# Routing weights applied at the experts' PSUM eviction, and an adding scatter into one row per token

## The chip, the cores and the metric

The kernel runs on one core of one Trainium2 chip. The metric is the device time of one execution in microseconds, and the figure for a kernel is the median of its runs. The profile shows one execution, taken by the hardware profiler. Its engines are PE (TensorE matmul), PEld (TensorE weight load), DVE (VectorE), ACT (ScalarE), POOL (GpSimd) and SP (SyncE, which issues most DMAs); 16 DMA engines move the data of all queues.

## The reference

One decoder block over 512 tokens of width 2048, in float32: a normalisation, a projection, 8 heads of forgetting attention beside 8 heads of chunkwise retention, gates, an output projection and a residual `h`. Behind it stands a mixture of 32 experts in 4 groups: each token takes one group, and in it the two best experts. Only this part is touched by the change:

```python
top_p, top_i = lax.top_k(e_prob, TOP_K)
top_p = top_p / jnp.sum(top_p, axis=-1, keepdims=True)
weights = p_group[:, None] * top_p
expert_id = g_sel[:, None] * EXPERTS_PER_GROUP + top_i
...
return (jax.nn.silu(xi @ w1[e]) * (xi @ w3[e])) @ w2[e]
...
yb = lax.map(expert_block, (xb, blk_expert)).reshape(cap, d) * buf_w[:, None]
return jnp.zeros((t_tok + 1, d), h.dtype).at[buf_tok].add(yb)[:t_tok]
```

The block's output is the normalised sum of `h` and this mixture. Each expert's matrices `w1`, `w3` (2048x512) and `w2` (512x2048) are 12.6 MB in float32, and all 32 are used.

## The kernel before

The program has four stages. Projections with both branches, then the output projection and the residual, run up to about 1420 us. The router follows, up to about 1441 us: it computes logits, the best group (`gm`, `ohg`), the best and second-best expert as one-hot arrays (`A1`, `A2`), and each token's rank in its expert (`rank1`, line 678). Then come the 32 experts, one after the other, and at the end the function `combine`, which adds everything up per token, normalises and stores.

**Experts.** The main loop is in lines 903 to 935. For each expert, `prep` (line 715) builds a 0/1 selection matrix `S` of tokens to 64 slots on POOL (expert 0 on DVE), and gathers the tokens' activations with matmuls of `h3` against `S` (line 737), in two halves; the halves are separate steps of a generator. A small matmul of `S` with the table `aux` (line 724, tile `ax`) carries a few numbers per slot: the token's inverse norm `rs`, its number, and whether this expert is its second choice. From them DVE computes `idx`, the row of the scatter (lines 755 to 760). `gemm1` (line 768) multiplies by `w1` and `w3`, `gated` (line 784) turns and gates the result, `gemm2` (line 798) multiplies by `w2`. The two halves of its output, `y`, are 128x512 tiles in PSUM: one is copied to `ysb` by ACT (line 815), the other by DVE (line 813). Then POOL issues an indirect DMA, the scatter (line 826), which writes the filled slots' rows of 4 KB into the DRAM tensor `ybuf`. That has 2 x 512 rows: row 2k holds token k's output of its best expert, row 2k+1 that of its second. Empty slots get a row number past the bound and are dropped. `ybuf` is set to zero earlier, by eight DMAs of 1 MB, one behind each attention head (line 332). The tile `ysb` has one buffer.

The last expert doesn't pass through `ybuf`. Its output is weighted (`wsl`), split in two float32r parts in `ys`, and put on the tokens by matmuls with the transposed selection `sT` (lines 817 to 823 and 960).

**Weights' stream.** SP loads the experts' matrices in pieces of 2 MB, six for each expert, into eight buffers that go round (`buffer`, line 702). The load of a piece waits until the matmuls on the buffer's last content are done. At the second-last expert two buffers are kept out of the round for `fw` and `ys` (lines 921 to 923).

**Routing weights.** `mixing` (line 870) computes them (`wt`: two numbers per token) on DVE with two Exp on ACT. The loop calls it at expert 12 and holds it behind that expert's gating. Its results are first read by `diagonals` (line 927) and by the last expert.

**combine** (line 940). Four loads of 2 MB bring `ybuf` back (lines 944 to 945); they stand on SP's queue behind the last weights and wait for the last scatter. For each of 4 tiles of 128 tokens and each of 4 blocks `c` of 512 columns, PE adds into PSUM three bfloat16 parts of `h` (line 957), the second choice's row times a diagonal matrix of its weight (line 959; left out for `c` = 0) and the last expert (line 960). DVE adds the first choice's row times its weight (line 961), and for `c` = 0 the second choice's as well (line 964). ACT sums the squares (line 966), POOL multiplies half of the blocks by the final norm's weight (line 968), DVE computes the inverse root in 13 small steps for each token tile, DVE and ACT scale (lines 976 and 978), and SP stores.

**Order.** On PE and SP the order of work is that of the program text. On DVE, ACT and POOL a planner sets the order, from a simulated timeline.

Of the kernel before, what the change touches and what calls it, by code (L numbers as in the profile page):

```python
# [11 lines left out]
F32 = mybir.dt.float32  # L12
F32R = mybir.dt.float32r
BF = mybir.dt.bfloat16
# [112 lines left out]
def hybrid_block(ctx, tc, a, out):  # L127
# [5 lines left out]
    def b3(ap, *shape):  # L133
        return ap.to_broadcast([P] + list(shape))
# [28 lines left out]
    c_d = dram.tile([H, T], F32, name="c_d")  # L163
    ybuf = dram.tile([2 * T, D], F32, name="ybuf")

# [126 lines left out]
    def fox_head(h, v):  # L292
# [38 lines left out]
        with tc.issue_after(done.ins):  # L331
            nc.scalar.dma_start(ybuf[h * P:(h + 1) * P].rearrange("p (a b) -> p a b", b=P),
                                zero[:, None, :].to_broadcast([P, D // P, P]))

# [130 lines left out]
    with pool("mtmp", 2, reuse_waits="tile") as mt:  # L465
        for j in range(KT):
            hi, lo = unit("br", j, after=done[3] if j == 1 else None)
            gs, bs = [], []
            for n in range(2):
# [4 lines left out]
                for k in range(H):  # L474
# [30 lines left out]
    tok2 = rp[0].tile([P, NT], F32, name="tok2")  # L505
    nc.gpsimd.iota(tok2, pattern=[[4 * P, NT]], base=0, channel_multiplier=0,
                   allow_small_or_imprecise_dtypes=True)
    par2 = rp[0].tile([P, NT], F32, name="par2")
    nc.gpsimd.iota(par2, pattern=[[0, NT]], base=0, channel_multiplier=4,
                   allow_small_or_imprecise_dtypes=True)  # L510
    aux = rp[0].tile([P, NT, 40], BF, name="aux")
    nc.gpsimd.memset(aux[:, :, 5:8], -8192.0)
    nc.gpsimd.tensor_copy(aux[:, :, 3], tok2)
# [176 lines left out]
    nc.gpsimd.dma_start(fwk, a["norm_final_w"].rearrange("o (k p) -> (o k) p", p=P))  # L690
    auxw = rp[0].tile([P, NT, 3], BF, name="auxw")

# [18 lines left out]
    rowbase = rp[0].tile([P, 1], F32, name="rowbase")  # L711
    nc.gpsimd.memset(rowbase[:SLOTS], 8192.0)
    nc.gpsimd.memset(rowbase[SLOTS:], 8193.0)

    def prep(rsel, is2, eng, late=False):

        S = cp.tile([P, NT, P], BF, name="S")
        for t in range(NT):
            i = eng.tensor_scalar(S[:, t], slot1.rearrange("p a b -> p (a b)"), rsel[:, t:t + 1], None,  # L719
                                  op0=OP.is_equal)  # L720
        gathering.append(i.ins)
        ax = psY.tile([P, 40], F32, name="ax", tag="y")
        for t in range(NT):
            nc.tensor.matmul(ax, S[:, t], aux[:, t], start=(t == 0), stop=(t == NT - 1))  # L724
        rs = cp.tile([P, 1], F32, name="rs", bufs=3)
        nc.vector.reduce_sum(rs, ax[:, 0:3], axis=AX.X)  # L726
        xs = cp.tile([P, KT, SLOTS], F32, name="xs")
        blk = [xs, rs, None]
        for g in range(2):
            if g:  # L730
                yield blk
            ks = slice(8 * g, 8 * g + 8)
            gp = psG.tile([P, 8, SLOTS], F32, name="gp")
            for d in range(8):
                for t in range(NT):
                    for i in range(3):
                        nc.tensor.matmul(gp[:, d], h3[i][:, t, (8 * g + d) * P:(8 * g + d + 1) * P],  # L737
                                         S[:, t, :SLOTS], start=(t == 0 and i == 0),
                                         stop=(t == NT - 1 and i == 2))
            nc.vector.tensor_mul(xs[:, ks], gp, b3(nfw[:, ks, None], 8, SLOTS))  # L740
        if late:
            ws = psY.tile([P, 3], F32, name="ws", tag="y")
            for t in range(NT):
                nc.tensor.matmul(ws, S[:, t], auxw[:, t], start=(t == 0), stop=(t == NT - 1))
            wsl = cp.tile([P, 1], F32, name="wsl", bufs=1)
            nc.vector.reduce_sum(wsl, ws, axis=AX.X)
            sp = psR.tile([P, NT, P], F32, name="tr")
            for t in range(NT):
                nc.tensor.matmul(sp[:, t], S[:, t], idb, start=True, stop=True)
            sT = cp.tile([P, NT, P], F32R, name="sT", bufs=1)  # L750
            nc.scalar.copy(sT, sp)
            blk[2] = wsl, sT
            yield blk
            return
        ix = cp.tile([P, 1], F32, name="ix", bufs=3)
        idx = cp.tile([P, 1], I32, name="idx", bufs=3)
        nc.vector.reduce_sum(ix, ax[:, 3:6], axis=AX.X)
        nc.vector.tensor_add(ix, ix, rowbase)
        nc.vector.scalar_tensor_tensor(idx, is2(ax[:, 8:40]), 2.0, ix, op0=OP.mult, op1=OP.add)
        blk[2] = idx  # L760
        yield blk
# [6 lines left out]
    def gemm1(blk, pieces, between=None):  # L768

        xs, rs, _ = blk  # L770
        acc = psA.tile([P, DE], F32, name="ab")
        for g in range(2):
            w = [next(pieces), next(pieces)]
            if g and between is not None:
                next(between)
            for kk in range(8):
                k = 8 * g + kk
                halves_mm(acc, xs[:, k], [w[m][:, kk * DE:(kk + 1) * DE] for m in range(2)],
                          k == 0, k == KT - 1)
        sb = cp.tile([P, DE], F32, name="ab", bufs=1)  # L780
        nc.scalar.activation(sb, acc, AF.Copy, scale=rs)  # L781
        return sb
# [15 lines left out]
    def gemm2(blk, pieces, ys=None):  # L798

        gs, (_, _, idx) = blk  # L800
        if ys is not None:
            wsl, sT = idx
        else:
            ysb = yp[0].tile([P, 2, DE], F32, name="ysb")
        w = [next(pieces), next(pieces)]
        for q in range(2):
# [4 lines left out]
            if ys is None:  # L811
                if q:
                    nc.vector.tensor_copy(ysb[:, q], y)
                else:
                    nc.scalar.copy(ysb[:, q], y)
                continue
# [7 lines left out]
        if ys is not None:  # L824
            return sT
        nc.gpsimd.indirect_dma_start(
            out=ybuf.rearrange("r (m n) -> (r m) n", m=2),
            out_offset=IndirectOffsetOnAxis(ap=idx[:, :1], axis=0),
            in_=ysb.rearrange("p q n -> p (q n)"), in_offset=None, bounds_check=4 * T - 1, oob_is_err=False)

# [39 lines left out]
    def mixing():  # L870
# [23 lines left out]
        for n in range(2):  # L894
            nc.vector.tensor_mul(wt[:, n], wt[:, n], wsum)
        wl, w2 = f("wl", NT), f("wl2", NT)
        nc.vector.tensor_mul(wl, wt[:, 0], A1.rearrange("p t g j -> p t (g j)")[:, :, NE - 1])
        nc.vector.tensor_mul(w2, wt[:, 1], A2[:, :, NE - 1])
        nc.vector.tensor_add(wl, wl, w2)
        split3(auxw, wl)  # L900
        return wt

    yp.append(scC.enter_context(pool("yout", 1, reuse_waits="tile")))
    nxt = prep_e(0)
    cur = next(nxt)
    for e in range(NE):
        sb = gemm1(cur, pieces_of(a["wM"][e], 0), None if e else nxt)
        if e == 8:
            with tc.issue_after(last_ins[-1].ins):
                nblk, eid, sta, en, it = extra_blocks()  # L910
        if e == 12:
            with tc.issue_after(last_ins[-1].ins):
                wtf = mixing()
        was = cur
# [11 lines left out]

    def diagonals():

        dgs = cp.tile([P, NT, P], F32, name="dgs", tag="ab", bufs=1)
        for t in range(NT):  # L930
            nc.gpsimd.tensor_scalar_mul(dgs[:, t], ident, wtf[:, 1, t:t + 1])
        return dgs

    dgs = diagonals()
    sT = gemm2((gs, was), pieces_of(a["wM"][NE - 1], 1), ys)


    yv = ybuf.rearrange("(t p k) d -> t p k d", p=P, k=2)

    def combine(dgs, first=False):  # L940

        def load_y(t):

            yb = buffer((P, 2, D))
            nc.sync.dma_start(yb, yv[t])
            return yb[:, 0], yb[:, 1]

        ybs = [load_y(t) for t in range(NT)] if first else None
        for t in range(NT):
            r, y1 = ybs[t] if first else load_y(t)  # L950
            dg = dgs[:, t]
            ss = small.tile([P, 4], F32, name="ss4")
            for c in (2, 3, 0, 1):
                cs = slice(c * T, (c + 1) * T)
                pr = psY.tile([P, T], F32, name="y") if c % 2 else psA.tile([P, T], F32, name="ab")
                for i in range(3):
                    nc.tensor.matmul(pr, idb, h3[i][:, t, cs], start=(i == 0), stop=False)
                if c:
                    nc.tensor.matmul(pr, dg, y1[:, cs], start=False, stop=False)
                nc.tensor.matmul(pr, sT[:, t], ys[:, cs], start=False, stop=True)  # L960
                nc.vector.scalar_tensor_tensor(r[:, cs], r[:, cs], wtf[:, 0, t:t + 1], pr,  # L961
                                               op0=OP.mult, op1=OP.add)
                if not c:
                    nc.vector.scalar_tensor_tensor(r[:, cs], y1[:, cs], wtf[:, 1, t:t + 1], r[:, cs],  # L964
                                                   op0=OP.mult, op1=OP.add)
                nc.scalar.activation(pr, r[:, cs], AF.Square, accum_out=ss[:, c:c + 1])
# [15 lines left out]

    combine(dgs, True)


    n_extra = nc.values_load(nblk[0:1, 0:1], min_val=0, max_val=MAXBLK)  # L986
    with tc.If(n_extra > 0):
        with tc.For_i(0, n_extra, 1):
# [27 lines left out]
            gemm2((gated(gemm1(blk, pieces_of(we, 0))), blk), pieces_of(we, 1))  # L1016
        combine(diagonals())
    scC.close()
# [70 lines left out]
```

## Time and profile before

| | |
|---|---|
| median of 3 runs | 2460.95 us (2460.93 to 2462.9) |
| the profiled execution | 2456.61 us, its span 2454.9 us |
| mean granted TensorE clock | 0.989 |
| busy share of the span | PE 96%, PEld 66%, DVE 30%, ACT 19%, POOL 10% |
| HBM read, written | 562.72 MB, 37.24 MB |
| experts' weights | 192 loads of 2048 KB |
| scatters | 31, median 10.5 us from issue to landing |
| loads of `ybuf` | 4 of 2048 KB |

The busy share of PE is high in every stage, so it doesn't tell which stage is bound by what: a matmul that waits a little before it starts still leaves PE nearly full. The busy share of the DMA engines tells the stages apart, and it is read per stretch of time. Times inside the span are given from its start.

### The profile page before, as it was taken

The page shows a single profiled execution, that of the slowest core. Times are in us where ns is not written, and L with a number is a line of the kernel's source. Part 1 is how long each engine was busy: PE and PEld are TensorE (multiplying, and loading weights), DVE is VectorE, ACT ScalarE, POOL GpSimd, SP SyncE. Part 2 cuts the span into 40 slices and gives each one's busy share as a digit, 9 for nine tenths or more (in the row PEclk, how much of TensorE's full clock was granted, in tenths as well). Part 3 has the DMA queues.
Part 4 walks back from the last instruction along what each step waited for, and adds up shares of the span by engine and source line. Part 5 has one row for each costly group of instructions (what it writes and reads, how often), then busy time and mean ns, then how long its engine had stood idle before and what let it go on. Part 6 is the DMA issues. An engine that isn't in the chain of part 4 may idle for free. (4 is left out here: it accounts for less than half of the span.)

```text
span 2454.9 us, 36000 instructions
## 1 busy us (share of the span) xinstructions
PE 2357.7 (96%) x16112; PEld 1618.9 (66%) x16114; DVE 725.4 (30%) x1269; ACT 471.3 (19%) x586; POOL 237.1 (10%) x330
## 2 busy tenths in 40 slices
PE   8999999999999999999999979999999999999996
PEld 6888888888888888888888854444444444444443
DVE  4444445543442222244433231101010000000005
ACT  5212223223222222232223310000010000000004
POOL 0000000100100000001003221111111111111102
PEclk9999999999999999999999989999999999999998
DMA  7233324232223332344432379999999999999995
GB/s 290 98 107 126 110 98 142 78 112 73 108 78 129 129 124 105 116 157 150 150 109 102 137 306 404 426 425 426 425 426 426 425 426 423 424 426 424 426 398 219
DMA packets 71439, 594.22 MB, mean 242 GB/s; under 512 B 8792, under 2 KB 25240, under 8 KB 37616
## 3 DMA queue, kind: packets, MB, share of 16 engines
q1 hardware_dynamic: 40320, 549.48, 54.8%
q0 software_dynamic: 9840, 25.61, 3.1%
q10 hardware_dynamic: 21120, 16.78, 2.1%
q8 instruction: 128, 2.10, 0.3%
q14 instruction: 31, 0.25, 0.0%
HBM read 562.72 MB, written 37.24 MB: 244 GB/s over the span
## 5 line engine op out<-in xcount | busy, mean ns | idle before, releaser
L766 PE MATMUL ab<-wraw,xs 128*64 128x512 f32 x2048 | 480.2, 602 | 40.6 <-DMA wraw<-in_wM_dram 38.9
L225 PE MATMUL acc<-xh,whl 128*128 128x512 f32 x1152 | 453.2, 393 | 0.0
L227 PE MATMUL acc<-xh,whl 128*128 128x512 f32 x1152 | 453.2, 393 | 0.0
L226 PE MATMUL acc<-xl,whl 128*128 128x512 f32 x1152 | 452.7, 393 | 0.0
L766 PEld LDWEIGHTS ab<-wraw,xs 128*64 128x64 f32 x2048 | 159.8, 139 | 353.9 <-issue 283.5
L96 ACT CAST whl<-wraw 128x2048 fp32r<-128x2048 f32 (+1 forms) x122 | 228.0, 1869 | 779.9 <-PE acc L227 412.5
L97 DVE TENSOR_TENSOR whl<-wraw,whl 128x2048 fp32r<-128x2048 f32 (+1 forms) x122 | 275.3, 2257 | 201.4 <-ACT whl L96 201.0
L226 PEld LDWEIGHTS acc<-xl,whl 128*128 128x128 f32 x1152 | 216.4, 188 | 46.6 <-issue 1.4
L227 PEld LDWEIGHTS acc<-xh,whl 128*128 128x128 f32 x1152 | 216.4, 188 | 45.7 <-issue 1.4
L225 PEld LDWEIGHTS acc<-xh,whl 128*128 128x128 f32 x1152 | 216.4, 188 | 45.6 <-issue 0.5
L766 PE MATMUL y<-wraw,gs 128*64 128x512 f32 x1024 | 229.1, 599 | 0.0
L737 PE MATMUL gp<-S,h 128*128 128x64 bf16 x6144 | 193.1, 193 | 16.1 <-issue 16.1
L737 PEld LDWEIGHTS <-h 128*128 128x128 bf16 x6144 | 187.9, 98 | 18.4 <-issue 18.1
L766 PEld LDWEIGHTS y<-wraw,gs 128*64 128x64 f32 x1024 | 71.1, 137 | 131.6 <-issue 129.9
L781 ACT ACTIVATE ab<-ab,rs 128x512 f32<-128x512 f32 x32 | 22.0, 688 | 619.6 <-PE ab L766 596.3
L726 DVE TENSOR_REDUCE rs<-ax 128x1 f32<-128x3 f32 x32 | 5.1, 160 | 459.1 <-PE ax L724 459.1
L719 POOL TENSOR_SCALAR S<-slot,rank 128x128 bf16<-128x128 f32 x124 | 73.3, 601 | 607.1 <-PE gp L737 600.5
L242 PE MATMUL acc<-whl,xh 128*128 128x512 f32 x256 | 101.6, 401 | 6.2 <-ACT xh L201 6.2
L243 PE MATMUL acc<-whl,xh 128*128 128x512 f32 x256 | 102.5, 400 | 0.9 <-DVE whl L97 0.9
L595 PE MATMUL acc<-whl,mh 128*128 128x512 f32 x256 | 100.4, 392 | 0.0
L596 PE MATMUL acc<-whl,mh 128*128 128x512 f32 x256 | 100.2, 391 | 0.0
L479 PE MATMUL acc<-oh,whl 128*128 128x512 f32 x256 | 99.4, 390 | 0.6 <-DVE whl L85 0.6
(303 smaller groups left out, 2061.9 us busy)
## 6 DMA issues: line engine op xcount, KB each, us to landing
wraw<-in_wM_dram SPq DMA_DIRECT2D x192, 2048.0 KB, 27.8
wraw<-in_wA_dram SPq DMA_DIRECT2D x59, 2048.0 KB, 7.7
ybuf<-zero ACTq DMA_DIRECT2D x8, 1024.0 KB, 5.9
gate<-gs ACTq DMA_DIRECT2D x32, 256.0 KB, 2.0
g<-gate POOLq DMA_DIRECT2D x32, 256.0 KB, 2.9
wraw<-ybuf SPq DMA_DIRECT2D x4, 2048.0 KB, 17.7
xt<-in_x_dram SPq DMA_DIRECT2D x4, 1024.0 KB, 6.9
hc<-in_x_dram POOLq DMA_DIRECT2D x4, 1024.0 KB, 5.5
```

The source lines that it names most:

```text
L96: nc.scalar.copy(hi[:, c], w[:, c])
L97: nc.vector.tensor_sub(lo[:, c], w[:, c], hi[:, c].bitcast(F32))
L225: nc.tensor.matmul(acc, wh, xh[:, k], start=(k == 0), stop=False)
L226: nc.tensor.matmul(acc, wh, xl[:, k], start=False, stop=False)
L227: nc.tensor.matmul(acc, wl, xh[:, k], start=False, stop=(k == KT - 1))
L242: nc.tensor.matmul(accs[t], xh[:, k, s], wh, start=(k == 0), stop=False)
L243: nc.tensor.matmul(accs[t], xh[:, k, s], wl, start=False, stop=False)
L479: nc.tensor.matmul(b, wl, oh[i], start=False, stop=(k == H - 1))
L595: nc.tensor.matmul(accs[t], mh[k][:, s], wh, start=(k == 0), stop=False)
L596: nc.tensor.matmul(accs[t], mh[k][:, s], wl, start=False, stop=False)
L737: nc.tensor.matmul(gp[:, d], h3[i][:, t, (8 * g + d) * P:(8 * g + d + 1) * P], S[:, t, :SLOTS], start=(t == 0 and i == 0), stop=(t == NT - ...
L766: nc.tensor.matmul(acc[m * SLOTS:(m + 1) * SLOTS], st, w[m], start=first, stop=last)
```

## The change

The DRAM tensor `ybuf` has one row per token instead of two. The scatter is issued with `compute_op=OP.add`: a row is added to what stands in `ybuf` instead of overwriting it. The two evictions of `y` multiply by the routing weight of each slot, `wsl`. So that the weight is there in time, `mixing` is called ahead of expert 0's first product; it writes the first choice's weight and the difference of the two weights, in three bfloat16 parts each, to six new columns of `aux`, and the small matmul `ax` carries them to the slots. That matmul moves from ahead of the gather's first half to ahead of its second half, and the steps on its result move behind the gather. `idx` loses the factor for the second choice. In `combine`, two loads of 2 MB replace four, the diagonal matrices with their matmuls and DVE's line 964 go, and DVE's line 961 becomes a plain addition. The zeroing of `ybuf` is halved: it stands behind every second head.

```diff
-    ybuf = dram.tile([2 * T, D], F32, name="ybuf")
+    ybuf = dram.tile([T, D], F32, name="ybuf")
...
-            nc.scalar.dma_start(ybuf[h * P:(h + 1) * P].rearrange("p (a b) -> p a b", b=P),
-                                zero[:, None, :].to_broadcast([P, D // P, P]))
+            if h % 2:
+                nc.scalar.dma_start(ybuf[h // 2 * P:(h // 2 + 1) * P].rearrange("p (a b) -> p a b", b=P),
+                                    zero[:, None, :].to_broadcast([P, D // P, P]))
...
-    aux = rp[0].tile([P, NT, 40], BF, name="aux")
+    aux = rp[0].tile([P, NT, 46], BF, name="aux")
...
-        ax = psY.tile([P, 40], F32, name="ax", tag="y")
-        for t in range(NT):
-            nc.tensor.matmul(ax, S[:, t], aux[:, t], start=(t == 0), stop=(t == NT - 1))
-        rs = cp.tile([P, 1], F32, name="rs", bufs=3)
-        nc.vector.reduce_sum(rs, ax[:, 0:3], axis=AX.X)
...
             if g:
                 yield blk
+                ax = psY.tile([P, 46], F32, name="ax", tag="y")
+                for t in range(NT):
+                    nc.tensor.matmul(ax, S[:, t], aux[:, t], start=(t == 0), stop=(t == NT - 1))
...
+        nc.vector.reduce_sum(rs, ax[:, 0:3], axis=AX.X)
+        nc.vector.reduce_sum(wd, ax[:, 40:46].rearrange("p (a b) -> p a b", a=2), axis=AX.X)
+        nc.vector.scalar_tensor_tensor(wsl, is2(ax[:, 8:40]), wd[:, 1:2], wd[:, 0:1], op0=OP.mult, op1=OP.add)
...
-        nc.vector.reduce_sum(ix, ax[:, 3:6], axis=AX.X)
-        nc.vector.tensor_add(ix, ix, rowbase)
-        nc.vector.scalar_tensor_tensor(idx, is2(ax[:, 8:40]), 2.0, ix, op0=OP.mult, op1=OP.add)
+            nc.vector.reduce_sum(ix, ax[:, 3:6], axis=AX.X)
+            nc.vector.tensor_add(idx, ix, rowbase)
...
-                    nc.vector.tensor_copy(ysb[:, q], y)
+                    nc.vector.tensor_scalar_mul(ysb[:, q], y, wsl)
                 else:
-                    nc.scalar.copy(ysb[:, q], y)
+                    nc.scalar.activation(ysb[:, q], y, AF.Copy, scale=wsl)
...
-            in_=ysb.rearrange("p q n -> p (q n)"), in_offset=None, bounds_check=4 * T - 1, oob_is_err=False)
+            in_=ysb.rearrange("p q n -> p (q n)"), in_offset=None, bounds_check=2 * T - 1, oob_is_err=False,
+            compute_op=OP.add)
...
-        wl, w2 = f("wl", NT), f("wl2", NT)
-        nc.vector.tensor_mul(wl, wt[:, 0], A1.rearrange("p t g j -> p t (g j)")[:, :, NE - 1])
-        nc.vector.tensor_mul(w2, wt[:, 1], A2[:, :, NE - 1])
-        nc.vector.tensor_add(wl, wl, w2)
-        split3(auxw, wl)
-        return wt
+        nc.vector.tensor_sub(wt[:, 1], wt[:, 1], wt[:, 0])
+        for n in range(2):
+            split3(aux[:, :, 40 + 3 * n:43 + 3 * n], wt[:, n])
...
     cur = next(nxt)
+    mixing()
     for e in range(NE):
         sb = gemm1(cur, pieces_of(a["wM"][e], 0), None if e else nxt)
...
-        if e == 12:
-            with tc.issue_after(last_ins[-1].ins):
-                wtf = mixing()
...
-    dgs = diagonals()
     sT = gemm2((gs, was), pieces_of(a["wM"][NE - 1], 1), ys)
...
+        for t in range(0, NT, 2):
             yb = buffer((P, 2, D))
-            nc.sync.dma_start(yb, yv[t])
-            return yb[:, 0], yb[:, 1]
+            nc.sync.dma_start(yb, ybuf.rearrange("(t p) d -> p t d", p=P)[:, t:t + 2])
+            ybs += [yb[:, 0], yb[:, 1]]
...
-                if c:
-                    nc.tensor.matmul(pr, dg, y1[:, cs], start=False, stop=False)
                 nc.tensor.matmul(pr, sT[:, t], ys[:, cs], start=False, stop=True)
-                nc.vector.scalar_tensor_tensor(r[:, cs], r[:, cs], wtf[:, 0, t:t + 1], pr,
-                                               op0=OP.mult, op1=OP.add)
-                if not c:
-                    nc.vector.scalar_tensor_tensor(r[:, cs], y1[:, cs], wtf[:, 1, t:t + 1], r[:, cs],
-                                                   op0=OP.mult, op1=OP.add)
+                nc.vector.tensor_add(r[:, cs], r[:, cs], pr)
```

## Rows read from the trace of the kernel before

**Rows 1.** The page, part 2: the span in 40 equal slices.

```profile
DMA  7233324232223332344432379999999999999995
```

**Rows 2.** Busy time by stretch: stretch, length, PE, PEld, DVE, ACT, POOL, PEclk, DMA share, GB/s.

```profile
1440.00:1460.00 20.00, 16.20 (x242) 10.54 (x244) 4.29 (x15) 0.00 (x0) 3.71 (x7) 0.83 0.29 104
...
2200.00:2300.00 100.00, 92.19 (x916) 41.94 (x914) 9.13 (x24) 4.97 (x9) 10.17 (x15) 0.98 1.01 425
2300.00:2350.00 50.00, 45.30 (x544) 22.73 (x542) 5.39 (x15) 3.32 (x6) 3.40 (x5) 1.00 0.96 404
2350.00:2370.00 20.00, 19.49 (x184) 8.56 (x181) 1.40 (x3) 0.77 (x2) 0.97 (x1) 1.00 0.96 390
...
2411.00:2448.00 37.00, 25.03 (x88) 11.01 (x88) 32.47 (x83) 18.77 (x44) 11.28 (x8) 0.89 0.34 138
```

**Rows 3.** Timeline, PE, from 2390 us: the last half of the last `gemm1`.

```profile
2390.08 7.08 PE L766 MATMUL ab<-wraw,xs 128*64 128x512 f32 x30 [2.33 <-DMA wraw<-in_wM_dram]
```

**Rows 4.** DMA queues from 1500 to 2380 us: packets, MB, share of 16 engines; issues.

```profile
q1 hardware_dynamic: 24974, 363.65, 97.5%
q0 software_dynamic: 4176, 7.64, 2.3%
...
ybuf<-ysb,idx POOLq DMA_INDIRECT x29, 10.5
```

**Rows 5.** Groups of instructions from 2411 to 2455 us: count, busy us, mean ns, idle.

```profile
L959 PE MATMUL y<-wraw,dgs 128*128 128x512 f32 x16 | 8.2, 592 | 0.0
L976 DVE SCALAR_TENSOR_TENSOR wraw<-wraw,rs_w 128x512 f32<-128x512 f32 x8 | 6.7, 873 | 0.1
...
L961 DVE SCALAR_TENSOR_TENSOR wraw<-wraw,wt,ab 128x512 f32<-128x512 f32 x8 | 5.9, 742 | 2.1 <-PE ab L960 1.9
L961 DVE SCALAR_TENSOR_TENSOR wraw<-wraw,wt,y 128x512 f32<-128x512 f32 x8 | 5.9, 737 | 0.6 <-PE y L960 0.6
...
L964 DVE SCALAR_TENSOR_TENSOR wraw<-wraw,wt 128x512 f32<-128x512 f32 x4 | 5.1, 1275 | 0.0
```

**Rows 6.** Timeline: an ACT eviction with a scale, a DVE product from PSUM.

```profile
1466.65 0.69 ACT L781 ACTIVATE ab<-ab,rs 128x512 f32<-128x512 f32 x1 [31.57 <-PE ab L766]
...
1788.87 0.69 DVE L740 TENSOR_TENSOR xs<-gp,nfw 128x512 f32<-128x512 f32 x1 [2.19 <-PE gp L737]
```

**Rows 7.** Timeline: `ybuf`'s loads on SP, and the first addition on DVE.

```profile
2392.53 4.98 SPq L945 DMA_DIRECT2D wraw<-ybuf  x4
...
2413.15 0.75 DVE L961 SCALAR_TENSOR_TENSOR wraw<-wraw,wt,ab 128x512 f32<-128x512 f32 x1 [1.92 <-PE ab L960]
```

**Rows 8.** Timeline: `mixing` beside expert 12, first and last of 27 on DVE, and ACT.

```profile
1790.09 0.16 DVE L874 TENSOR_TENSOR pgx<-L,fm1m 128x16 f32<-128x16 f32 x1
...
1796.50 0.17 DVE L686 TENSOR_TENSOR auxw<-s,auxw 128x4 bf16<-128x4 f32 x1
...
1789.74 1.28 ACT L875 ACT_TABLE_LOAD   x1
```

**Rows 9.** Timeline of the start of expert 0, PE and DVE.

```profile
1441.85 0.29 DVE L678 SCALAR_TENSOR_TENSOR rank<-rk,A 128x128 f32<-128x128 f32 x1 [0.67 <-PE rk L676]
...
1447.91 0.69 DVE L740 TENSOR_TENSOR xs<-gp,nfw 128x512 f32<-128x512 f32 x1 [3.74 <-PE gp L737]
...
1442.52 0.92 PE L724 MATMUL ax<-aux,S 128*128 128x40 bf16 x4 [0.77 <-DVE S L719]
1443.26 4.61 PE L737 MATMUL gp<-S,h 128*128 128x64 bf16 x96
...
1455.68 2.97 PE L737 MATMUL gp<-S,h 128*128 128x64 bf16 x96
```

**Rows 10.** Timeline: a scatter on POOL, and the next write to `ysb` on ACT.

```profile
1771.85 1.04 POOL L826 DMA_INDIRECT ybuf<-ysb,idx  x1 [5.99 <-issue]
...
1795.77 0.59 ACT L815 COPY ysb<-y 128x512 f32<-128x512 f32 x1 [3.74 <-PE y L766]
```

**Rows 11.** Landing times of the 18 scatters from 1440 to 2000 us (line 826).

```profile
DMA to landing us min/median/max: 10.1/10.4/11.4
```

More of the change, by code (lines that the diff above doesn't have):

```diff
@@ L505, in hybrid_block @@
     tok2 = rp[0].tile([P, NT], F32, name="tok2")
-    nc.gpsimd.iota(tok2, pattern=[[4 * P, NT]], base=0, channel_multiplier=0,
+    nc.gpsimd.iota(tok2, pattern=[[2 * P, NT]], base=0, channel_multiplier=0,
                    allow_small_or_imprecise_dtypes=True)
     par2 = rp[0].tile([P, NT], F32, name="par2")
-    nc.gpsimd.iota(par2, pattern=[[0, NT]], base=0, channel_multiplier=4,
+    nc.gpsimd.iota(par2, pattern=[[0, NT]], base=0, channel_multiplier=2,
                    allow_small_or_imprecise_dtypes=True)
-    aux = rp[0].tile([P, NT, 40], BF, name="aux")
-    nc.gpsimd.memset(aux[:, :, 5:8], -8192.0)
+    aux = rp[0].tile([P, NT, 46], BF, name="aux")
+    nc.gpsimd.memset(aux[:, :, 5:8], -4096.0)
     nc.gpsimd.tensor_copy(aux[:, :, 3], tok2)
@@ L690, in hybrid_block @@
     nc.gpsimd.dma_start(fwk, a["norm_final_w"].rearrange("o (k p) -> (o k) p", p=P))
-    auxw = rp[0].tile([P, NT, 3], BF, name="auxw")
     cp = scC.enter_context(pool("cx", 2, reuse_waits="tile"))
@@ L711, in hybrid_block @@
     rowbase = rp[0].tile([P, 1], F32, name="rowbase")
-    nc.gpsimd.memset(rowbase[:SLOTS], 8192.0)
-    nc.gpsimd.memset(rowbase[SLOTS:], 8193.0)
+    nc.gpsimd.memset(rowbase[:SLOTS], 4096.0)
+    nc.gpsimd.memset(rowbase[SLOTS:], 4097.0)
     def prep(rsel, is2, eng, late=False):
@@ L721, in prep @@
         gathering.append(i.ins)
-        ax = psY.tile([P, 40], F32, name="ax", tag="y")
-        for t in range(NT):
-            nc.tensor.matmul(ax, S[:, t], aux[:, t], start=(t == 0), stop=(t == NT - 1))
-        rs = cp.tile([P, 1], F32, name="rs", bufs=3)
-        nc.vector.reduce_sum(rs, ax[:, 0:3], axis=AX.X)
         xs = cp.tile([P, KT, SLOTS], F32, name="xs")
-        blk = [xs, rs, None]
+        blk = [xs, None, None, None]
         for g in range(2):
@@ L740, in prep @@
             nc.vector.tensor_mul(xs[:, ks], gp, b3(nfw[:, ks, None], 8, SLOTS))
-        if late:
[L742 to L746, printed above, removed]
+        rs = cp.tile([P, 1], F32, name="rs", bufs=3)
+        ix = cp.tile([P, 1], F32, name="ix", bufs=1)
+        idx = cp.tile([P, 1], I32, name="idx", bufs=3)
+        wd = cp.tile([P, 2], F32, name="wd", bufs=1)
+        wsl = cp.tile([P, 1], F32, name="wsl", bufs=3)
+        nc.vector.reduce_sum(rs, ax[:, 0:3], axis=AX.X)
+        nc.vector.reduce_sum(wd, ax[:, 40:46].rearrange("p (a b) -> p a b", a=2), axis=AX.X)
+        nc.vector.scalar_tensor_tensor(wsl, is2(ax[:, 8:40]), wd[:, 1:2], wd[:, 0:1], op0=OP.mult, op1=OP.add)
+        blk[1:] = rs, wsl, idx
+        if late:
             sp = psR.tile([P, NT, P], F32, name="tr")
@@ L751, in prep @@
             nc.scalar.copy(sT, sp)
[L752 to L756, printed above, removed]
-        nc.vector.reduce_sum(ix, ax[:, 3:6], axis=AX.X)
-        nc.vector.tensor_add(ix, ix, rowbase)
-        nc.vector.scalar_tensor_tensor(idx, is2(ax[:, 8:40]), 2.0, ix, op0=OP.mult, op1=OP.add)
-        blk[2] = idx
+            blk[3] = sT
+        else:
+            nc.vector.reduce_sum(ix, ax[:, 3:6], axis=AX.X)
+            nc.vector.tensor_add(idx, ix, rowbase)
         yield blk
@@ L768, in gemm1 @@
     def gemm1(blk, pieces, between=None):
-        xs, rs, _ = blk
+        xs = blk[0]
         acc = psA.tile([P, DE], F32, name="ab")
@@ L780, in gemm1 @@
         sb = cp.tile([P, DE], F32, name="ab", bufs=1)
-        nc.scalar.activation(sb, acc, AF.Copy, scale=rs)
+        nc.scalar.activation(sb, acc, AF.Copy, scale=blk[1])
         return sb
@@ L798, in gemm2 @@
     def gemm2(blk, pieces, ys=None):
[L800 to L803, printed above, removed]
+        gs, (_, _, wsl, idx) = blk
+        if ys is None:
             ysb = yp[0].tile([P, 2, DE], F32, name="ysb")
@@ L824, in gemm2 @@
         if ys is not None:
-            return sT
+            return idx
         nc.gpsimd.indirect_dma_start(
@@ L925, in hybrid_block, with combine @@
     spread_fw(fw)
-    def diagonals():
-        dgs = cp.tile([P, NT, P], F32, name="dgs", tag="ab", bufs=1)
-        for t in range(NT):
-            nc.gpsimd.tensor_scalar_mul(dgs[:, t], ident, wtf[:, 1, t:t + 1])
-        return dgs
-    dgs = diagonals()
[L935 to L944, printed above, removed]
-            nc.sync.dma_start(yb, yv[t])
-            return yb[:, 0], yb[:, 1]
[L948 to L951, printed above, removed]
+    sT = gemm2((gs, was), pieces_of(a["wM"][NE - 1], 1), ys)
+    def combine():
+        ybs = []
+        for t in range(0, NT, 2):
+            yb = buffer((P, 2, D))
+            nc.sync.dma_start(yb, ybuf.rearrange("(t p) d -> p t d", p=P)[:, t:t + 2])
+            ybs += [yb[:, 0], yb[:, 1]]
+        for t in range(NT):
+            r = ybs[t]
             ss = small.tile([P, 4], F32, name="ss4")
@@ L981, in combine @@
                 nc.sync.dma_start(out[t * P:(t + 1) * P, cs], r[:, cs])
-    combine(dgs, True)
+    combine()
     n_extra = nc.values_load(nblk[0:1, 0:1], min_val=0, max_val=MAXBLK)
@@ L1016, in hybrid_block @@
             gemm2((gated(gemm1(blk, pieces_of(we, 0))), blk), pieces_of(we, 1))
-        combine(diagonals())
+        combine()
     scC.close()
```

## The prediction

> **What bounds the kernel now.** I read the slices of the span first. The busy share of the DMA engines is 1 to 4 tenths up to the router, but for the first slice, and then 9 tenths almost to the end [rows 1]. So there are two kernels in one, and the change touches only the second. The stretches come next: in a hundred microseconds of the experts' stage the DMA share is 1.01 at 425 GB/s, while PE is busy for 92 of 100 us [rows 2]. PE has some 8% to spare there, DVE 90% and ACT 95%. The stage lasts as long as its bytes take. At its start it is different: in the first 20 us the DMA share is 0.29 [rows 2], since the buffers are full and PE has not yet begun to free them. A late start of PE there moves everything behind it. That the stage ends on a DMA shows in the last half of the last `gemm1`, which begins at 2390.08 us after 2.33 us of waiting for a weight [rows 3]. From there some 65 us are left: the last expert's arithmetic, and from 2411 us on `combine`, where DVE is busy 32.5 of 37 us, PE 25 and the DMA engines a third of the time [rows 2]. There DVE is the bound.
>
> So an edit counts if it changes the bytes of the experts' stage, the start of PE at expert 0, or DVE's work in `combine`. The change does something to all three.
>
> **The scatter adds.** The queues of 1500 to 2380 us [rows 4] are the main view. The weights' queue moved 363.65 MB at 97.5% of 880 us, 858 us, so 424 GB/s. The scatters' queue moved 7.64 MB in 29 scatters, 0.263 MB each, at 2.3%, 20.2 us, or 0.70 us each. The shares add up to a full stage: a scatter isn't hidden beside the weights but takes their place. To add, something has to read the old row: the scatter's bytes are now read twice and written once. The trace has no adding DMA, so I bound the cost. Below: nothing, if an engine fetches the old row while it is busy with the other side of the transfer. Above: the old row is fetched and the sum written as passes of their own, two more scatters' worth, 2 x 0.70 = 1.40 us. Between the ends I take one more read of the same bytes at the rate at which the weights are read from the same memory, 0.263 MB / 424 GB/s = 0.62 us, since a read from HBM into the engines is what these rows show most of. 30 of the 31 scatters are issued before 2390 us: 30 x 0.62 = 18.6 us. From 2300 to 2370 us the DMA share is 0.96 [rows 2], so 2.8 us are free there, and the two or three scatters in it can put about 1 us into them. **+17.6 us**, with ends at 0 and 30 x 1.40 = +42 us.
>
> The Trainium skill, "Collectives: The Full Stack", in the section on the bandwidth ceiling, says that an add in a DMA costs no cycles of its own but needs two source reads on the same read ring, and measures a reduction at 1/1.93 of a copy's rate. By that ratio each scatter would cost 0.93 x 0.62 = 0.58 us more, the term +17 us; no run here shows it yet.
>
> **combine.** DVE loses line 964, 5.1 us in four instructions [rows 5]. They run at 1.275 us, 0.74 being the price of the like line 961, so they were stretched by something beside them. Line 961, 16 times at 0.74 us, becomes an addition of a PSUM operand; the nearest row, a product of the same shape from PSUM, takes 0.69 us [rows 6]: 16 x 0.05 = 0.8 us. Together 5.9 us from an engine that is the bound, but in the first microseconds it waits for PE [rows 5, 7], so I take **-5.5 us**. If only the unstretched price comes back (4 x 0.74) and nothing else, -3; if the other stretched lines relax too (line 976 runs at 0.873), up to -8. PE loses the 24 passes of line 959, 16 of them at 8.2 us busy, so some 12 of its 25 us [rows 2, 5]: nothing, as DVE ends later. What is late next is still DVE, with some 26 us, ahead of ACT's 19 [rows 2].
>
> **Loads of ybuf.** Two of 2 MB instead of four. The first tile's data still comes with the first 2 MB; it was issued at 2392.53 us and DVE first adds at 2413.15 [rows 7]. The saved 4 MB lie behind it, under a DMA share of 0.34 [rows 2]: nothing. The cover is some 3 us: if the last scatter lands later, this load starts later, but then alone on the engines, with 2.1 MB / 424 GB/s = 5 us for 2 MB.
>
> **mixing moved to the front.** Beside expert 12 it took 27 DVE instructions from 1790.09 to 1796.67 us, and a table load of 1.28 us on ACT [rows 8]. The new one has three less for the last expert's weight, one subtraction and four splits more: 29, some 7 us. At the start DVE is free from about 1443 us on but for 0.7 us at 1447.9, and the first reader is now `ax` of expert 0 ahead of the gather's second half at 1455.68 us [rows 9]. 12 us of room for 7: nothing. PE's queue waits behind that `ax`, so what is over the room would be paid in full; and if the planner put all of it ahead of `rank`, the start would be 7 us later. On the other side `ax` itself leaves the front of the first gather: 1443.26 - 1442.52 = 0.74 us [rows 9] earlier. I take **0**, with ends at -0.7 and +7.
>
> **At nothing.** The evictions with a scale: ACT does one in 0.69 us [rows 6] against 0.59 for the copy [rows 10], and PE is not the bound. The new reductions for `wsl`: some four DVE instructions of 0.16 us for each expert, under 90% of idle DVE. `ax` in its new place: it shares PSUM buffers with `y`, and its readers are done about 1 us after the gather, well before the second `y`. The table of `aux`: 46 columns for 40. The halved zeroing: ACT's queue in the attention, at a DMA share of 2 to 4 tenths [rows 1]. Also gone are the four POOL products of `diagonals`, off the path.
>
> **Sum.** 17.6 - 5.5 + 0 = +12.1 us. On the profiled execution, 2456.6 us (span 2454.9 and 1.7 around it), that is 2468.7. That execution is 4.3 us below the median of the runs, 2460.95, so I put the difference on the median: **2473 us**. The limit of what a measurement of this kernel can tell from no change is about 0.2%, 4.9 us.
>
> **Rivals.**
> *The added read is hidden.* If an engine reads the old row beside its write, only `combine` is left: 2460.95 - 5.5 = 2455.5 us, faster. For it speaks that reading and writing are different directions; against it that in [rows 4] the scatters and the weights, which go in opposite directions, already share the engines' time without overlap. With a part of the read hidden, 0 to 10 us of the 17.6, the result is between 2456 and 2466.
> *Two passes more.* 42 - 1 - 5.5 = +35 us: 2496. For it speaks that the scatter is already dearer for its bytes than the weights (0.70 against 0.62 us); against it, nothing seen.
> *The landing becomes a wait.* `ysb` has one buffer; ACT writes it again 24 us after the scatter's issue [rows 10], and a scatter lands in 10.4 us [rows 11]. A landing up to twice as long is covered. Beyond 24 us ACT waits, PE's next `y` behind it, and after PE's spare time, 8% of 30 us, each microsecond is paid 30 times. At 30 us of landing: (30 - 24 - 2.4) x 30 = 108 us, 2580. It takes an adding row that blocks its queue for a round trip.
> The Trainium skill, "DMA: Bandwidth & Descriptors", section on two DMAs through the same engine, reports that the second of two adding packets read stale data when it directly followed the first; so they don't wait for each other's round trip, which speaks against this case. No run here shows it.
> *The start.* mixing ahead of the first gather: 2473 + 7 = 2480.
>
> **How the numbers follow.** One more read: 0.55, with its own band of 2466 (the start 0.7 earlier, `combine` at -8, the read 15% cheaper) to 2481 (the late start). Hidden read: 0.13, half of it under 2456. Partly hidden: 0.11. Two passes: 0.16, from 2482 to 2502. The landing: 0.05. Faster by over 0.2% is the whole hidden read and a bit of its neighbour: 0.11. Within 0.2%, 2456 to 2466: 0.13. Slower: 0.76. The range leaves out the landing, the top of the two passes and the best of the hidden reads: 2455 to 2497.
>
> **What would show it.** Right: the weights' loads still fill the stage at a DMA share of 1, the last half of the last `gemm1` starts some 18 us later than 2390, the scatters' queue takes about twice its 2.3%, and from there to the end it is 5 to 6 us shorter, with DVE at about 26 us. A landing of 12 to 20 us. Wrong: a stage of the same length (the read was hidden), a stage longer by 40 (passes of their own), ACT waiting at `ysb` for the scatter (the landing), or a first gather later than 1443 us (mixing). If DVE's time in `combine` falls and the end doesn't, something else was behind it.

## The result, and the profile after

The changed kernel takes 2471.53 us (median of 5 runs, 2470.84 to 2475.24), the kernel before 2460.93 us (5 runs beside it): slower, with a ratio of 1.0051 and a 95% interval of 1.0039 to 1.0062, which is 10 to 15 us. The forecast was 2473 us. The profiled executions have spans of 2469.0 and 2454.9 us, 14.1 us apart; the profiled execution of the kernel before is one of its quickest, 4.3 us under its median, that of the changed kernel 0.7 under its own, so the two differences don't agree. First the stretches of the changed kernel (stretch, length, PE, PEld, DVE, ACT, POOL, PEclk, DMA share, GB/s):

```profile
2200.00:2300.00 100.00, 90.77 (x974) 42.96 (x971) 10.12 (x31) 5.27 (x9) 14.15 (x19) 0.98 1.00 416
...
2409.00:2413.00 4.00, 3.90 (x12) 1.18 (x14) 0.00 (x0) 0.00 (x0) 0.00 (x0) 0.57 0.99 404
```

The experts' stage is as full of DMA as before [rows 2], but the engines carry 416 GB/s where they carried 425. They are busy with something that isn't counted in the bytes. The queues from 1500 to 2380 us say which one (packets, MB, share of 16 engines):

```profile
q1 hardware_dynamic: 24468, 356.36, 95.4%
q0 software_dynamic: 4139, 7.57, 4.4%
```

The scatters' queue moves nearly the same bytes as in [rows 4] and takes 4.4% instead of 2.3% of the engines' time; the weights lose what it gains. Then the marks by which the span can be cut, from PE's timeline: the last half of the last `gemm1`, and the first product of `combine`.

```profile
2409.10 8.78 PE L763 MATMUL ab<-wraw,xs 128*64 128x512 f32 x30 [3.86 <-DMA wraw<-in_wM_dram]
...
2432.11 0.59 PE L935 MATMUL ab<-h,idb 128*128 128x512 bf16 x2 [0.16 <-issue]
```

The second mark in the kernel before:

```profile
2411.43 0.59 PE L957 MATMUL ab<-h,idb 128*128 128x512 bf16 x2 [0.16 <-issue]
```

Up to the first mark 19.0 us are lost (2390.08 before [rows 3]). Between the marks it is 23.0 us, 1.7 more than before. From the second mark to the end it is 36.9 us, where before it was 43.5 (2411.43 to 2454.9): 6.6 gained. 19.0 + 1.7 - 6.6 = 14.1, so the whole difference has its place. `combine` has three pieces: from PE's first product to DVE's first addition, from there to DVE's last instruction, and the last stores behind it. The middle one, before and after (stretch, length, PE, PEld, DVE, ACT, POOL, PEclk, DMA share, GB/s):

```profile
2413.15:2448.39 35.24, 23.04 (x81) 10.11 (x80) 32.62 (x82) 17.36 (x42) 11.28 (x8) 0.88 0.31 122
...
2432.97:2461.82 28.85, 15.47 (x59) 6.53 (x58) 24.86 (x78) 18.17 (x43) 10.96 (x8) 0.80 0.24 94
```

DVE stands idle for only 2.6 of these 35.2 us before and for 4.0 of 28.9 after, while PE is busy for 23.0 and 15.5: this piece is nearly all DVE's own busy time, which fell by 7.8 us. DVE's groups from 2432 us to the end, with PE's part gone and no line 964 [rows 5]:

```profile
L937 DVE TENSOR_TENSOR wraw<-wraw,ab 128x512 f32<-128x512 f32 x8 | 5.5, 684 | 2.6 <-PE ab L936 2.3
L937 DVE TENSOR_TENSOR wraw<-wraw,y 128x512 f32<-128x512 f32 x8 | 5.4, 681 | 1.6 <-PE y L936 1.5
```

The plain addition takes 0.68 us, as the row of a like product said [rows 6]. The start, with `mixing` moved to it (DVE's `rank`, `mixing`'s last instruction, then PE):

```profile
1441.83 0.29 DVE L679 SCALAR_TENSOR_TENSOR rank<-rk,A 128x128 f32<-128x128 f32 x1
...
1446.52 0.18 DVE L687 TENSOR_TENSOR aux<-s,aux 128x4 bf16<-128x4 f32 x1
...
1442.50 5.11 PE L735 MATMUL gp<-S,h 128*128 128x64 bf16 x96 [0.70 <-DVE S L719]
...
1455.48 0.27 PE L729 MATMUL ax<-aux,S 128*128 128x46 bf16 x4
```

The planner began `mixing` at 1437.24 us, inside the chain that leads to `rank`, and yet `rank` comes at the same time as before (1441.85 [rows 9]). `mixing` ends 9 us before `ax` reads its result. Last the scatters' landing from 1440 to 2000 us, and one scatter with the next write to `ysb`:

```profile
DMA to landing us min/median/max: 11.2/12.1/12.8
```

```profile
1563.86 1.59 POOL L821 DMA_INDIRECT ybuf<-ysb,idx  x1 [6.06 <-issue]
...
1587.32 0.69 ACT L810 ACTIVATE ysb<-y,wsl 128x512 f32<-128x512 f32 x1 [7.50 <-PE y L763]
```

A landing of 12 us [10.4 before, rows 11] is far under the 22 to 24 us that pass before `ysb` is written again. POOL's instruction grew from 1.04 [rows 10] to 1.59 us, which nothing waits for.

### The profile page after: what moved, and what is told of

It is laid out like the page before. It is cut to its first block, busy times and chain, and to the rows that moved or that the text cites. A ratio compares the mean times of both kernels' runs of the same rounds, so it can differ in the third digit from the quotient of the medians.

```text
span 2469.0 us, 35981 instructions
## 1 busy us (share of the span) xinstructions
PE 2357.4 (95%) x16084; PEld 1616.2 (65%) x16086; DVE 717.8 (29%) x1299; ACT 472.9 (19%) x585; POOL 251.1 (10%) x326
## 4 chain that ended last, share of the span: by engine, by line
PE 79%; DMA 17%; DVE 1%; issue 1%; ACT 1%; SPq 0%; POOL 0%; DVEq 0%; POOLq 0%; ACTq 0%
DMA wraw<-in_wM_dram 17%; PE ab L763 12%; PE acc L226 11%; PE acc L225 11%; PE acc L227 11%; PE y L763 5%; PE gp L735 5%; PE acc L598 2%; PE acc L596 2%; PE acc L597 2%; PE acc L480 2%; PE acc L479 2%; PE acc L478 2%; PE acc L243 2%; PE acc L244 2%; PE acc L242 2%
## 5 line engine op out<-in xcount | busy, mean ns | idle before, releaser
L763 PE MATMUL ab<-wraw,xs 128*64 128x512 f32 x2048 | 488.2, 612 | 52.9 <-DMA wraw<-in_wM_dram 51.2
L738 DVE TENSOR_TENSOR xs<-gp,nfw 128x512 f32<-128x512 f32 x64 | 44.3, 692 | 624.1 <-PE gp L735 624.1
```

Source lines behind the costliest of these rows:

```text
L763: nc.tensor.matmul(acc[m * SLOTS:(m + 1) * SLOTS], st, w[m], start=first, stop=last)
```

## The experiments

Every kernel was timed beside the kernel before on the same chips, whose median in these sets was 2459.0 to 2460.2 us. Differences are of medians, intervals of ratios.

**The change without its add.** The scatter writes; which of a token's two rows stays is left to their order.

```diff
-            compute_op=OP.add)
```

> The changed kernel with its scatter writing instead of adding: the add of a token's two rows is left out. One more read of each scatter's bytes (my theory): the weights' stage shrinks by 30 x 0.62 = 18.6 us, the scatters' queue goes back from 4.4% to about 2.3% of 1500 to 2380 us, the last half of the last gemm1 starts near 2390 us again, and against the kernel before only the shorter combine is left: some 2455 us, 5 to 7 under before. Rival, the stage is longer because of what stands beside the add (scaled evictions, the moved small matmul, mixing at the start): it stays within 3 us of the changed kernel's 2471.5.

It takes 2451.06 us: 8.3 us under the kernel before, 0.9969 (0.9957 to 0.9982), a little more than expected. It is 20.5 us under the changed kernel by the medians, which are of different sets, and 18.9 by each one's difference to the kernel before. Its queue's row from 1500 to 2380 us is that of the kernel before, and the last half of the last `gemm1` starts where it did there (2390.08 [rows 3]):

```profile
q0 software_dynamic: 4176, 7.64, 2.3%
...
2389.89 8.78 PE L763 MATMUL ab<-wraw,xs 128*64 128x512 f32 x30 [2.41 <-DMA wraw<-in_wM_dram]
```

So all that the change loses hangs on the one operation, and everything else in it together is a gain. The rival, that the scaled evictions, the moved matmul or `mixing` lengthen the stage, falls.

**The add alone.**

```diff
-            in_=..., in_offset=None, bounds_check=4 * T - 1, oob_is_err=False)
+            in_=..., in_offset=None, bounds_check=4 * T - 1, oob_is_err=False,
+            compute_op=OP.add)
```

> The kernel before, whose scatter adds to its zeroed rows instead of writing them; nothing else is changed, and two rows per token stay. My theory: 18 to 19 us slower than before, some 2479 us, the scatters' queue at 4.4%, combine as long as before. Rival, that two experts' adds to one row hinder each other in the changed kernel: here, with a row of its own for each output, the loss is clearly smaller than 18 us.

2480.23 us, 20.9 more than before, 1.0086 (1.0072 to 1.0099), somewhat more than the 18 to 19 expected. The queues from 1500 to 2380 us:

```profile
q1 hardware_dynamic: 24472, 356.43, 95.4%
q0 software_dynamic: 4122, 7.52, 4.4%
```

Here no two experts add to the same row, and the price is the same as with shared rows: it isn't a collision of adds. The queue takes 2.1% of 880 us, 18.5 us, more than the plain scatter: 0.64 us for each of 29.

**One more transfer of the same bytes, first try.** A copy of 64 rows of 4 KB within DRAM behind each scatter's line in the program.

```diff
...
+        nc.gpsimd.dma_start(more, a["x"][:SLOTS, :2 * DE])
```

> The kernel before with one more DMA behind each scatter: 64 rows of 4 KB (0.262 MB) copied from x to an unused place in DRAM. If an add costs what one more transfer of the same bytes costs (my theory): 31 x 0.62 to 0.70 us, 18 to 22 us slower than before, as slow as the kernel before with the add alone. Rival, the add costs something of its own beyond the bytes: this kernel is clearly less slow than that one, by 5 us or more.

2472.72 us, 13.4 more, 1.0058 (1.0044 to 1.0073). It would have spoken for the rival, but the trace shows that the copies never ran in the stage. POOL's order is the planner's, nothing held them back, and it issued all of them in the first 164 us; the experts' stage then started late (the second row, from 1440 us: PE is busy 8 of 20 us where it was 16 [rows 2]). This run says nothing on the price of a transfer.

```profile
L831 POOL DMA_DIRECT2D more<-in_x_dram x31: 501/501/549, 5.4 to 163.5; - x31
...
1440.00:1460.00 20.00, 8.09 (x76) 6.89 (x76) 15.17 (x53) 4.06 (x10) 10.43 (x16) 0.59 0.90 383
```

**The same, held in place.**

```diff
...
+        with tc.issue_after(sc.ins):
+            nc.gpsimd.dma_start(more, a["x"][:SLOTS, :2 * DE])
```

> The kernel before with a copy of 64 rows of 4 KB (0.262 MB) from x to an unused place in DRAM, held behind each scatter. If an add costs what one more transfer of the same bytes costs (my theory): 18 to 22 us slower than before, as the add alone was (20.9), and the shares of the two queues in the stage as in that kernel. Rival, the add costs something beyond the bytes: this kernel loses clearly less than 18 us.

2477.53 us, 18.5 more, 1.0077 (1.0064 to 1.009). Queues from 1500 to 2380 us:

```profile
q1 hardware_dynamic: 24449, 356.08, 95.5%
q0 software_dynamic: 6367, 14.88, 4.3%
```

**The scatter twice.** A second scatter of the same rows, without an add, into another tensor.

```diff
+        nc.gpsimd.indirect_dma_start(
+            out=ybuf2.rearrange("r (m n) -> (r m) n", m=2),
...
+            in_=ysb.rearrange("p q n -> p (q n)"), in_offset=None, bounds_check=4 * T - 1, oob_is_err=False)
```

> The kernel before with each scatter issued a second time, without adding, into another DRAM tensor of the same shape. My theory: an add costs one more pass of the same rows, so this loses as much as the add alone did, 19 to 22 us (31 x 0.62 to 0.70), with the scatters' queue at 4.6% of the stage. Rival, that the add is the cheaper of the two, since it generates one set of rows instead of two: this one loses over 25 us. A wait at the single output buffer, which both scatters now hold, would show as idle time of ACT at line 815 that ends on a DMA.

2481.53 us, 22.5 more, 1.0093 (1.008 to 1.0106): just above the expected band, and under the rival's 25. ACT's waits at its line `ysb<-y` end on PE, 30 of 31, so the single buffer made no wait. Its queue's row:

```profile
q0 software_dynamic: 8170, 14.76, 4.4%
```

Three kernels, three ways to fill the queue: an add 0.64 us, a copy of the same bytes 0.61 (2.0% of 880 us over 29), a second scatter 0.64. The intervals of their ratios overlap. An add costs here what one more transfer of its bytes costs; no difference can be told. One thing differs: with copy or second scatter the queue's megabytes double, with the add they stay at 7.5. The trace counts an added row once; that the second pass is the reading of the old row is inferred from its price, it isn't shown.

**Line 964's work moved to PE.** In `combine`, PE adds the second choice's rows in all four blocks, and line 964 goes.

```diff
-                if c:
+                if True:
                     nc.tensor.matmul(pr, dg, y1[:, cs], start=False, stop=False)
...
-                if not c:
-                    nc.vector.scalar_tensor_tensor(r[:, cs], y1[:, cs], wtf[:, 1, t:t + 1], r[:, cs],
-                                                   op0=OP.mult, op1=OP.add)
```

> The kernel before, with the second choice's rows added by PE for all four blocks, so that DVE's line 964 goes and nothing else: PE gets 4 x 0.86 = 3.4 us more. If DVE bounds combine and line 964 is most of what the change took from it (my theory): 4 to 6 us faster than before, 2454 to 2456. Rival, PE or the wait for the loads of ybuf is close behind DVE in combine: less than 3 us faster, since PE ends later by 3.4 us.

2461.52 us, 2.5 more than before, 1.0011 (1.0002 to 1.002): the expectation fell, and the rival's condition held, as PE got 3.4 us of work more. DVE's groups from 2410 us to the end, and the stretch from DVE's first addition to its last instruction:

```profile
L117 DVE SCALAR_TENSOR_TENSOR rs_t<-rs_w,v 128x1 f32<-128x1 f32 x12 | 6.0, 502 | 0.4
L961 DVE SCALAR_TENSOR_TENSOR wraw<-wraw,wt,ab 128x512 f32<-128x512 f32 x8 | 5.9, 742 | 3.0 <-PE ab L960 2.9
L961 DVE SCALAR_TENSOR_TENSOR wraw<-wraw,wt,y 128x512 f32<-128x512 f32 x8 | 5.9, 741 | 1.7 <-PE y L960 1.6
...
L122 DVE TENSOR_TENSOR rs_w<-rs_w,rs_t 128x1 f32<-128x1 f32 x12 | 3.3, 272 | 0.3
...
2412.65:2450.05 37.40, 26.49 (x89) 11.63 (x88) 30.99 (x78) 17.40 (x42) 10.53 (x8) 0.91 0.29 115
```

DVE's busy time fell by 1.6 us only (from 32.62), though line 964's 5.1 us are gone, and its idle time grew from 2.6 to 6.4 us. Of the idle time, 2.0 us are more waiting for PE at line 961 (4.5 where it was 2.5 [rows 5]). Of the busy time, much went to small instructions: line 117 takes 6.0 us in twelve where it took 4.3, line 122 3.3 where it took 2.4. Line 117 takes 0.22 us or, as here, up to 1.22. The timeline of this kernel shows what runs beside it:

```profile
2438.05 1.22 DVE L117 SCALAR_TENSOR_TENSOR rs_t<-rs_w,v 128x1 f32<-128x1 f32 x1
...
2437.99 1.27 POOL L965 TENSOR_TENSOR wraw<-wraw 128x512 f32<-128x512 f32 x1 [4.04 <-ACT ab L963]
```

The DVE instruction ends with POOL's product. In the kernel before, POOL's products fell on line 964 above all, and on line 117 less often. Line 964 takes 0.74 us at 2425.22, just as POOL's product from 2424.01 on ends, and 1.73 beside one:

```profile
2417.39 1.28 POOL L968 TENSOR_TENSOR wraw<-wraw 128x512 f32<-128x512 f32 x1 [1.04 <-ACT y L966]
2417.49 1.73 DVE L964 SCALAR_TENSOR_TENSOR wraw<-wraw,wt 128x512 f32<-128x512 f32 x1
```

So the stretch isn't a property of line 964; it falls on whichever such instruction is there. What taking line 964 away would give with PE's work unchanged, no run shows. The Trainium skill, "SBUF — State Buffer", section "Who interferes with whom", says that a DVE instruction with two SBUF inputs contends with a POOL instruction that reads SBUF, and one with at most one, outside the 2-port perf modes, doesn't. The trace agrees: lines 117 and 964 have all their inputs in SBUF, and line 961, with one of its two tensors in PSUM, keeps its 0.74 us in both kernels.

**PE's part alone, and both parts.** Two kernels that leave work of the second choice out: the first without PE's products (its rows are missing in three of four blocks), the second without line 964 as well (they are missing altogether).

```diff
-                if c:
-                    nc.tensor.matmul(pr, dg, y1[:, cs], start=False, stop=False)
```

> The kernel before without PE's line 959: the second choice's rows are left out of three of the four column blocks, DVE's line 964 stays. If combine was held by DVE alone, as the prediction had it: within 2 us of before, since DVE's work is the same. Rival (my theory after the last run): PE and DVE end together in combine, PE's products delay the first additions of each tile, and both have to shrink: 2 to 4 us faster.

> The kernel before without line 959 and line 964: the second choice's rows are loaded and then left out altogether. PE and DVE both shrink, as in the change, with the weighted addition of line 961 kept. If both engines' parts are what the change took out of combine: 6 to 8 us faster than before, as the changed kernel without the add was (8.3 us). Rival, that the halved loads of ybuf or the moved weights made part of that: clearly less than 6 us.

Without PE's part 2455.32 us, 4.9 less than before, 0.9981 (0.9972 to 0.999). Without both 2451.09 us, 9.1 less, 0.9968 (0.9957 to 0.9979), as much as the changed kernel gains without its add (0.9969). Both are more than was expected. So PE's products are worth 4.9 us, and line 964 another 4.2 once they are gone: together they are what `combine` gained. Why PE's products are worth so much is another question, and the trace doesn't bear out that PE and DVE end together. Without PE's part, the stretch from DVE's first addition to its last instruction and DVE's groups; the last row is line 117 in the kernel before:

```profile
2415.23:2446.17 30.94, 15.60 (x59) 6.56 (x58) 29.00 (x82) 18.23 (x43) 10.07 (x8) 0.84 0.24 96
...
L959 DVE SCALAR_TENSOR_TENSOR wraw<-wraw,wt,ab 128x512 f32<-128x512 f32 x8 | 6.0, 745 | 1.6 <-PE ab L958 1.5
L962 DVE SCALAR_TENSOR_TENSOR wraw<-wraw,wt 128x512 f32<-128x512 f32 x4 | 6.0, 1488 | 0.0
L959 DVE SCALAR_TENSOR_TENSOR wraw<-wraw,wt,y 128x512 f32<-128x512 f32 x8 | 5.9, 739 | 0.8 <-PE y L958 0.6
L974 DVE SCALAR_TENSOR_TENSOR wraw<-wraw,rs_w 128x512 f32<-128x512 f32 x8 | 5.6, 745 | 0.0
L117 DVE SCALAR_TENSOR_TENSOR rs_t<-rs_w,v 128x1 f32<-128x1 f32 x12 | 2.8, 246 | 0.0
...
L117 DVE SCALAR_TENSOR_TENSOR rs_t<-rs_w,v 128x1 f32<-128x1 f32 x12 | 4.3, 362 | 0.2
```

DVE waited for PE for 2.5 us before and waits for 2.1 now, so that isn't where the gain lies. DVE's busy time fell by 3.6 us, from 32.62 to 29.00, with the same 82 instructions: line 976 (here 974) went from 6.7 to 5.6 us and line 117 from 4.3 to 2.8, while line 964 (here 962) rose from 5.1 to 6.0. The first addition also comes 0.9 us sooner behind PE's first product (2414.37 here). Without PE's part other instructions stand beside POOL's products. The planner lays DVE's instructions in another order in each of these kernels; how much of the 3.6 us is due to that, and how much to PE's quicker pace, wasn't tried.

**Adding where the DMA engines have room.** Two rows per token and a plain scatter, as before; weights at the eviction and the short `combine`, as in the change; the two rows are added on the way back, by a DMA into SBUF behind the last weights.

```diff
...
+            nc.sync.dma_start(yb, yv[t, :, 0])
+            nc.gpsimd.dma_start(yb, yv[t, :, 1], accum_op=OP.add)
...
```

> The changed kernel with two rows per token and a plain scatter, as before; combine loads the first choice's rows and adds the second choice's by a DMA into SBUF that adds, behind the last scatter, where the DMA engines have room. My theory: the stage is as long as before and combine as short as after the change: some 2455 us, faster than both kernels. Rival, the adds become the wait at the end: four loads and four adds are 8.4 MB, 12.6 MB with the added reads, 30 us at 424 GB/s from 2392 us on, so the last token tile may come only at 2422 us or later, and each microsecond that combine waits is lost: 2460 us or more.

2454.11 us: 5.2 less than before, 0.9977 (0.9968 to 0.9986), and 16 to 17 less than the changed kernel. It beats both. The adds do come late: they are issued from 2402.88 us on, each behind its plain load, and DVE's first addition stands at 2416.09 us, 3.5 us behind PE's first product at 2412.56, where the changed kernel had 0.9 (2432.97 behind 2432.11). But the DMA engines were idle for two thirds of `combine` before, and are at 0.69 of their time now:

```profile
2402.88 0.98 POOL L927 DMA_DIRECT2D wraw<-ybuf  x1 [20.37 <-DMA wraw<-ybuf]
...
2412.60:2448.80 36.20, 15.15 (x66) 6.62 (x64) 25.90 (x78) 18.82 (x44) 11.46 (x9) 0.81 0.69 199
```

Its median is 3 us above the version without any add (2451.06). The intervals of the two overlap, but the later first addition, 2.7 us, is of the same size: the adds with their loads cost some 3 us where they stand.

## Why the prediction was right

**The add** was forecast at one more read of each scatter's bytes, 0.62 us, and +17.6 us. It is 0.64 us in the queue's share, 30 x 0.64 = 19.2, and 19.0 us at the last half of the last `gemm1`; by the runs with and without it 18.9 to 20.9 us. One read, between the ends of 0 and 1.40, was the right choice, but the kernel before had no adding DMA to read it from: it was the likeliest case, and the runs settled it. The 1 us that free DMA time at 2350 to 2370 us was to take in didn't come. The gap in the stream moved with the stage and got no smaller: by the shares the engines were idle for 3.3 us of 2340 to 2360 us before (0.76 and 0.91 in its two halves), and are for 3.9 us of 2360 to 2370 us now (0.61). The Trainium skill, "Collectives: The Full Stack", section on the bandwidth ceiling, has a reduction at 1/1.93 of a copy's rate; this trace agrees, 4.4% against 2.3% being 1.91. The prediction set that ratio against the weights' 0.62 us and came to 0.58; against the scatter's own 0.70 it gives an estimate of 0.65, nearer to the 0.64 measured.

**combine** was forecast at -5.5 us. In the profiled executions it is -6.6, in the runs without the add -8.3, the edge of the range that was given for it. That DVE bounds `combine` was right: it is idle for 2.6 of 35.2 us before and 4.0 of 28.9 after. Two terms of it were sized wrong. The first is the price of DVE's instructions. The sum took 5.9 us from it, and its busy time fell by 7.8 (32.62 to 24.86), for the sum held fixed prices, while part of that time is spent beside POOL's products. The prediction saw such a stretch in line 964 and allowed up to -8 for it. The second is PE's 12 us, put at nothing "as DVE ends later". Leaving PE's products out alone gains 4.9 us, though DVE does end later: the first addition comes 0.9 us sooner and DVE's own instructions get 3.6 us shorter, in the profiled executions. DVE waited longer for PE after the change (3.8 us at the additions, before 2.5), and that took back some of it.

**The loads of ybuf, mixing, the moved matmul, the evictions** were put at nothing and cost nothing that the trace shows: the first product of expert 0 comes at 1442.50 us (`ax`, then the first, at 1442.52 before [rows 9]) and its `rank` stands where it stood, and the version without the add is as fast as the one that only leaves the second choice out.

**Not foreseen** were the 1.7 us between the marks. The last half of `gemm1` takes 8.78 us where it took 7.08 [rows 3], since PE's granted clock is 0.57 from 2409 to 2413 us, mostly the lower of its two levels, after a wait of 3.86 us. The length of the wait doesn't decide it. The version without the add waited 2.41 us and took 8.78 as well, and the one without PE's products waited 2.32 and took 8.78; the kernel before waited 2.33 and took 7.08, and the one with the early copies waited 2.40 and took 7.08. Each is one execution. What does decide was not settled.

The sum, +12.1 us, stands between the two measured differences, 10.6 of the medians and 14.1 of the profiled executions. In the profiled executions the add was put 1.4 us too low, `combine` gained 1.1 more than forecast, and the 1.7 us between the marks were missing; by the medians the errors of the two main terms, 1.3 to 3.3 and 2.8 us, went against each other. That they partly cancelled is luck. The rivals of a hidden read, of two passes, of a wait for the landing and of a late start have all fallen, the first two by the queue's share, the third by the landing, the last by the start's rows.

## What to carry to other kernels

In a stage that the DMA engines fill, count a DMA that adds as a second pass of its bytes, as it was here, however few instructions it saves elsewhere. Where the engines have room, try the add there: here that cost some 3 us instead of 19 to 21. An instruction's time isn't a fixed price: on a busy engine it may hold a wait for another engine, and what an edit takes away can come back in the next instruction or bring more than its own time, so read the engine's whole busy time before and after. And look where the planner put an instruction that nothing holds back, before a result is read from it.

## What the runs showed of the hardware

An adding DMA's bytes are counted once by the trace, while its queue's share of the engines doubles (7.5 MB at 4.4% against 7.6 MB at 2.3%): the rate falls, 416 GB/s at a full share where 425 stood, and that is the sign of it. The page's HBM read doesn't show it either: 562.72 MB before and with the add alone. The landing grows only from 10.4 to 12.1 us, by a sixth, and so tells little of a price that doubled. And a DVE instruction on one number per partition, 0.22 us by itself, takes 1.22 us beside a POOL product of 1.27 us.
